# A two-layer encoder on one core: products of ones at the opening, another order of the first casts and loads, a sum moved to VectorE, and the last columns in two runs

## The chip, the core and the metric

The kernel runs on one core of a Trainium2 chip. A core has five engines that each work through their own list of instructions: TensorE (PE in the profile; its weight loads are PEld), VectorE (DVE), ScalarE (ACT), GpSimd (POOL) and SyncE (SP), which here only starts DMA transfers. ScalarE and GpSimd start transfers too (rows ACTq and POOL DMA). The metric is the device time of one execution in microseconds.

## The reference

Two layers work on 256 tokens of 1024 features in float32. Each normalises its input, projects it with one large matrix `w_in` to queries, keys and values of two mixers and to gates, runs both mixers, merges them with sigmoid gates and projects the result back with `w_out`, with a residual. A last normalisation closes.

```python
def rmsnorm(x, w):
    xf = x.astype(jnp.float32)
    y = xf * lax.rsqrt(jnp.mean(xf * xf, axis=-1, keepdims=True) + EPS)
    return y.astype(x.dtype) * w

for l in range(DEPTH):                      # DEPTH = 2
    h = rmsnorm(x, norm_w[l])
    proj = h @ w_in[l]                      # 1024 x 10272
    (q_a, k_a, v_a, ab_a, z_a, q_b, k_b, v_b, z_b,
     gate_a, gate_b) = jnp.split(proj, SPLIT_IDX, axis=-1)
    y_a = gated_delta_branch(q_a, k_a, v_a, ab_a, z_a, ...)   # short convolution, gated delta rule
    y_b = diff_attention_branch(q_b, k_b, v_b, z_b, ...)      # differential attention
    merged = (jax.nn.sigmoid(gate_a) * (y_a @ w_pa[l])
              + jax.nn.sigmoid(gate_b) * (y_b @ w_pb[l]))
    x = x + merged @ w_out[l]
return rmsnorm(x, final_norm_w)
```

## The kernel before

The 256 tokens are two token tiles of 128 (`m` is 0 or 1), the 1024 features eight slices of 128 (`kt`). Every projection is made of column groups of 512. A product in full precision is made of three in the faster format: both operands are split into a high and a low part, and high x high, high x low and low x high are summed in PSUM. So each group of 512 columns takes 2 x 8 x 3 = 48 products of 128 x 128 by 512.

`weights` (L207) loads such a group in four weight blocks (`kp` 0 to 3, 512 KB each, two `kt` in each), casts each to the high part on ScalarE (L230) and subtracts it from the original on VectorE for the low part (L232). The tile `raw` of a load comes free once its low part is made; three such tiles go round, so the fourth load waits for the first subtraction. `later` names an instruction behind which a block's cast or subtraction is to be placed, `held` one behind which its load is issued, on ScalarE's queue instead of SyncE's. `behind(ins)` does the placing: what stands under it is put later in order than `ins`. All else is ordered by a planner that builds each engine's list from a simulated timeline.

`proj_by_tile` (L259) makes the first projection of a layer (group `vb`, tile names `pp_vb`) and the last (`pp_o`) token tile by token tile: all 24 products of tile 0 (L282), then `evac`, then tile 1. For the opening of layer 0, `between` (L363) interleaves this with the norm of the tokens: the load of block 1 goes behind the first square of token tile 0, that of block 2 behind block 0's cast, block 3 by SyncE, and token tile 1's norm follows. The loads after these in the opening are `wab` (L468, behind the cast of block 2, on ScalarE's queue), `cwr` (the rows of the convolution weights, 120 x 128 numbers, L413, on SyncE's queue), and the weights of the k group (`raw_k`, SyncE's).

A norm (`normed`, L172) squares two halves of 512 columns on ScalarE with a sum along the row (L169), adds the two sums and EPS on GpSimd (L164), raises to the power -0.5 on GpSimd (L165), and scales on VectorE (L179). `split_T` (L184) turns the result on TensorE (four transposes of 128 x 128, L189), casts it to the high part on ScalarE (L195) and makes the low part on VectorE (L196); the result is `hT`. In layer 0 the norm's weights come to all rows by a product of one row of ones with the weights' row (`norm_row`, L145, PSUM tile `wb_n`).

At the end, the residual of token tile 1 is added (L1015), squared, summed and raised as above, ScalarE scales the first 512 columns (L1045), VectorE the last (L1046), and two transfers carry the rows out (L1048).

## Time and profile before

| what | value |
|---|---|
| time, median of 3 runs | 779.53 us (779.36 to 779.75) |
| span of the profiled execution, first to last instruction | 777.1 us |
| TensorE busy | 758.2 us, 98% |
| VectorE, ScalarE, GpSimd busy | 557.3, 474.9, 101.9 us |
| DMA | 126.91 MB, mean 163 GB/s |

The page gives the profiled execution by its span; the runs' times take in 2.4 us more, what lies around the first and last instruction. The rows of the timeline give start, length, engine, line, operation, written tile <- read tiles, shapes, and in brackets the idle time before and what ended it. A row of n instructions (xn) spans all of them. The chain of waits follows the work that ended last back to the start: each piece is what the next one waited for.

### The profile page before, as it was taken

The page shows a single profiled execution, that of the slowest core. Times are in us where ns is not written, and L with a number is a line of the kernel's source. Part 1 is how long each engine was busy: PE and PEld are TensorE (multiplying, and loading weights), DVE is VectorE, ACT ScalarE, POOL GpSimd, SP SyncE. Part 2 cuts the span into 40 slices and gives each one's busy share as a digit, 9 for nine tenths or more (in the row PEclk, how much of TensorE's full clock was granted, in tenths as well). Part 3 has the DMA queues.
Part 4 walks back from the last instruction along what each step waited for, and adds up shares of the span by engine and source line. Part 5 has one row for each costly group of instructions (what it writes and reads, how often), then busy time and mean ns, then how long its engine had stood idle before and what let it go on. Part 6 is the DMA issues. An engine that isn't in the chain of part 4 may idle for free.

```text
span 777.1 us, 13805 instructions
## 1 busy us (share of the span) xinstructions
PE 758.2 (98%) x5222; PEld 647.7 (83%) x5222; DVE 557.3 (72%) x1051; ACT 474.9 (61%) x1042; POOL 101.9 (13%) x137
## 2 busy tenths in 40 slices
PE   8999999999999999999999999999999999999996
PEld 4899879887778888887889888899777788888784
DVE  5686878999974635377677776989999553536782
ACT  5657776557677744564554668655577776356551
POOL 5100461100030100010010025510001110001000
PEclk9999999999999999999999999999999999999998
DMA  7752756554496644346664256755446954343631
GB/s 227 240 177 78 224 146 198 174 172 136 112 207 187 210 135 129 117 144 210 215 224 136 82 160 221 194 170 161 141 137 174 233 164 160 114 133 111 213 110 54
DMA packets 77745, 126.91 MB, mean 163 GB/s; under 512 B 19679, under 2 KB 20015, under 8 KB 77680
## 3 DMA queue, kind: packets, MB, share of 16 engines
q1 hardware_dynamic: 71038, 112.99, 48.4%
q0 software_dynamic: 3936, 9.77, 4.8%
q10 hardware_dynamic: 2706, 3.28, 1.3%
q8 instruction: 41, 0.67, 0.4%
q14 instruction: 24, 0.20, 0.1%
HBM read 121.27 MB, written 4.75 MB: 162 GB/s over the span
## 4 chain that ended last, share of the span: by engine, by line
PE 81%; DVE 7%; DMA 5%; ACT 4%; issue 2%; POOL 0%; SPq 0%; POOLq 0%; ACTq 0%; DVEq 0%
PE pp_vb L282 5%; DMA raw_q<-in_w_in_dram 3%; PE pp_qk L245 2%; PE pp_qk L246 2%; PE pp_qk L244 2%; PE pp_o L282 2%; PE pf_k L298 2%; PE pf_k L302 2%; PE pf_v L298 2%; PE pf_k L300 2%; PE pp_gb L245 2%; PE sc L839 2%; PE pp_gb L244 2%; PE pf_v L302 2%; PE pf_v L300 2%; PE av L865 2%
## 5 line engine op out<-in xcount | busy, mean ns | idle before, releaser
L245 PE MATMUL pp_qk<-lo_qk,hT 128*128 128x512 f32 x128 | 51.3, 401 | 1.0 <-DVE lo_qk L232 1.0
L246 PE MATMUL pp_qk<-hi_qk,hT 128*128 128x512 f32 x128 | 50.1, 391 | 0.0
L230 ACT CAST hi_qk<-raw_qk 128x1024 fp32r<-128x1024 f32 x32 | 33.5, 1046 | 23.6 <-PE pp_qk L246 12.6
L244 PE MATMUL pp_qk<-hi_qk,hT 128*128 128x512 f32 x128 | 46.1, 398 | 0.7 <-ACT hi_qk L230 0.7
L232 DVE TENSOR_TENSOR lo_qk<-raw_qk,hi_qk 128x1024 fp32r<-128x1024 f32 x32 | 40.2, 1257 | 7.6 <-ACT hi_qk L230 7.4
L232 DVE TENSOR_TENSOR lo_pb<-raw_pb,hi_pb 128x1024 fp32r<-128x1024 f32 x16 | 19.6, 1224 | 35.7 <-ACT hi_pb L230 35.7
L298 PE MATMUL pf_q<-hT,hi_q 128*128 128x256 f32 x128 | 36.5, 288 | 0.3 <-ACT hi_q L230 0.2
L298 PE MATMUL pf_v<-hT,hi_v 128*128 128x256 f32 x128 | 36.5, 289 | 0.0
L300 PE MATMUL pf_v<-hT,hi_v 128*128 128x256 f32 x128 | 36.2, 286 | 0.0
L300 PE MATMUL pf_q<-hT,hi_q 128*128 128x256 f32 x128 | 35.9, 284 | 0.0
L848 ACT ACTIVATE es<-sc,mx 128x256 f32<-128x256 f32 x64 | 29.8, 473 | 10.1 <-DVE mx L846 10.0
L298 PE MATMUL pf_k<-hT,hi_k 128*128 128x256 f32 x128 | 35.8, 285 | 0.0
L302 PE MATMUL pf_q<-hT,lo_q 128*128 128x256 f32 x128 | 35.7, 292 | 0.0
L300 PE MATMUL pf_k<-hT,hi_k 128*128 128x256 f32 x128 | 35.7, 283 | 0.0
L232 DVE TENSOR_TENSOR lo_gb<-raw_gb,hi_gb 128x1024 fp32r<-128x1024 f32 x16 | 19.6, 1224 | 22.2 <-ACT hi_gb L230 22.0
L232 DVE TENSOR_TENSOR lo_ga<-raw_ga,hi_ga 128x1024 fp32r<-128x1024 f32 x16 | 19.6, 1226 | 21.0 <-ACT hi_ga L230 21.0
L302 PE MATMUL pf_v<-hT,lo_v 128*128 128x256 f32 x128 | 34.6, 286 | 0.0
L302 PE MATMUL pf_k<-hT,lo_k 128*128 128x256 f32 x128 | 34.4, 285 | 0.0
L230 ACT CAST hi_pb<-raw_pb 128x1024 fp32r<-128x1024 f32 x16 | 16.8, 1049 | 25.1 <-PE pp_pb L246 24.3
L527 DVE SCALAR_TENSOR_TENSOR cvq<-pf_q,cw,cvq 128x254 f32<-128x254 f32 (+1 forms) x64 | 29.7, 476 | 1.8 <-ACT cvq L523 1.4
L527 DVE SCALAR_TENSOR_TENSOR cvv<-pf_v,cw,cvv 128x254 f32<-128x254 f32 (+1 forms) x64 | 30.2, 483 | 0.6 <-ACT cvv L523 0.5
L527 DVE SCALAR_TENSOR_TENSOR cvk<-pf_k,cw,cvk 128x254 f32<-128x254 f32 (+1 forms) x64 | 28.5, 478 | 2.0 <-ACT cvk L523 1.3
(356 smaller groups left out, 2495.5 us busy)
## 6 DMA issues: line engine op xcount, KB each, us to landing
raw_qk<-in_w_in_dram SPq DMA_DIRECT2D x32, 512.0 KB, 3.7
raw_k<-in_w_in_dram SPq DMA_DIRECT2D x16, 512.0 KB, 4.6
raw_q<-in_w_in_dram SPq DMA_DIRECT2D x16, 512.0 KB, 3.7
raw_v<-in_w_in_dram SPq DMA_DIRECT2D x16, 512.0 KB, 3.8
raw_zb<-in_w_in_dram SPq DMA_DIRECT2D x16, 512.0 KB, 3.6
raw_za<-in_w_in_dram SPq DMA_DIRECT2D x16, 512.0 KB, 3.7
raw_gb<-in_w_in_dram SPq DMA_DIRECT2D x16, 512.0 KB, 4.7
raw_o<-in_w_out_dram SPq DMA_DIRECT2D x16, 512.0 KB, 4.5
```

Of the source, the lines that this page charges most:

```text
L230: high = S.copy(hi[:, :, :n], raw[:, :, :n]).ins
L232: mark[nm, kp] = high, V.tensor_tensor(lo[:, :, :n], raw[:, :, :n], hi[:, :, :n].bitcast(F32), ALU.subtract).ins
L244: T.matmul(o, act[kt // 4][:, 0, kt % 4, ts_], hi, start=kt == 0, stop=False)
L245: T.matmul(o, act[kt // 4][:, 0, kt % 4, ts_], lo, start=False, stop=False)
L246: mark["proj"] = T.matmul(o, act[kt // 4][:, 1, kt % 4, ts_], hi, start=False, stop=kt == KT - 1).ins
L282: mark["proj"] = T.matmul(o, a_, w_, start=kt == 0 and a_ is ah and w_ is hi, stop=kt == KT - 1 and a_ is al).ins
L298: T.matmul(o, hi[:, cs], act[kt // 4][:, 0, kt % 4, :], start=first, stop=False, skip_group_check=True)
L300: T.matmul(o, hi[:, cs], act[kt // 4][:, 1, kt % 4, :], start=False, stop=False, skip_group_check=True)
L302: T.matmul(o, lo[:, cs], act[kt // 4][:, 0, kt % 4, :], start=False, stop=done, skip_group_check=True)
L527: V.scalar_tensor_tensor(ca[:, o0:o1], acc[:, b, o0 + sft : o1 + sft], cw[:, j, cb : cb + 1], ca[:, o0:o1], ALU.mult, ALU.add)
L839: mm = T.matmul(sp[n][:, qt * SEQ : (qt + 1) * SEQ], qkT[h // 4][rows, 0, h % 4, qt * P : (qt + 1) * P], qkT[h // 4][rows, 1, h % 4, :], s ...
L848: S.activation(es[:, n, qt, :], spv[:, qt, :], AF.Exp, bias=mx[:, n, qt : qt + 1], accum_out=s_all[:, h, n, qt : qt + 1])
```

## The change

Seven edits:

- `ones`, a tile of 128 x 128, is filled on VectorE before the first load, and TensorE multiplies it by itself five times into a PSUM tile that nobody reads.
- The sum of the two mean squares and EPS goes from GpSimd to VectorE, placed behind the same instruction as the squares.
- In layer 0's first projection, block 0 is cast and subtracted in two halves of one `kt` each (`fine`), and its casts are placed behind the cast of the first half of token tile 0 (`split, 0, 0`). Block 2's load and others that name block 0's cast now name its second half.
- In layer 0, the load of the convolution's rows is placed behind the load of block 3 of the first projection.
- In the last projection of layer 1, token tile 1 (`cut`) is made in two runs of 256 columns, each with all 24 products and a residual add of its own.
- The final norm of token tile 1 follows these runs: behind the first, its square, a sum on GpSimd and the product with the weights; behind the second, square, sum on VectorE, power, and the scaling, in which VectorE scales the two quarters by two instructions.
- The tile of the row sums has three columns instead of two.

```diff
     def norm_factor(xt_, m, h, r, ss, halves_, after=None):
...
-        G.tensor_scalar(r, ss[:, 0:1], ss[:, 1:2], EPS, ALU.add, ALU.add)
+        with behind(after):
+            V.tensor_scalar(r, ss[:, 1:2], ss[:, 0:1], EPS, ALU.add, ALU.add)
         mark["pow"] = G.tensor_tensor(r, r, mhalf[:, :1], ALU.pow).ins
...
                 with behind(load):
-                    (nc.scalar if load else nc.sync).dma_start(
+                    mark[nm, "load"] = (nc.scalar if load else nc.sync).dma_start(
                         out=raw[:, :, :n],
...
-                with behind(act):
-                    high = S.copy(hi[:, :, :n], raw[:, :, :n]).ins
-                with behind(dve):
-                    mark[nm, kp] = high, V.tensor_tensor(lo[:, :, :n], raw[:, :, :n],
-                                                         hi[:, :, :n].bitcast(F32), ALU.subtract).ins
+                for ks in ((slice(0, 1), slice(1, 2)) if kp in fine else (slice(0, 2),)):
+                    with behind(act):
+                        high = S.copy(hi[:, ks, :n], raw[:, ks, :n]).ins
+                    with behind(dve):
+                        mark[nm, kp] = high, V.tensor_tensor(lo[:, ks, :n], raw[:, ks, :n],
+                                                             hi[:, ks, :n].bitcast(F32), ALU.subtract).ins
...
-        parts = weights(w, c0, 512, nm, places, ahead=False, later=later, spare=spare, held=held)
+        parts = weights(w, c0, 512, nm, places, ahead=False, later=later, spare=spare, held=held,
+                        fine=(0,) if between else ())
...
+            if m in cut:
+                for c_ in range(2):
+                    cs = slice(256 * c_, 256 * c_ + 256)
+                    for kt in range(KT):
+                        hi, lo = (w_[:, cs] for w_ in ws[kt][1:])
+                        ah, al = (act[kt // 4][:, part, kt % 4, ts_] for part in range(2))
+                        for a_, w_, n_ in ((ah, hi, 0), (ah, lo, 1), (al, hi, 2)):
+                            with behind(mark.get("proj")):
+                                mark["proj"] = T.matmul(o[:, cs], a_, w_, start=kt == 0 and n_ == 0,
+                                                        stop=kt == KT - 1 and n_ == 2).ins
+                    evac(m, o, cs)
+                    yield
+                continue
...
+    ones = work.tile([P, P], F32, tag="sqj", name="ones", bufs=1)
+    V.memset(ones, 1.0)
+    idle = bank_c("idle")
+    for _ in range(5):
+        T.matmul(idle[:, :P], ones, ones, start=True, stop=True)
     wb = norm_row(norm_w[0], "n0")
...
-            later[0] = None, mark["norm", 0][1]
+            later[0] = mark["split", 0, 0][0], mark["norm", 0][1]
...
-        nc.sync.dma_start(out=cw_rows, in_=conv_w[l].rearrange("t (b c) -> (t b) c", c=P))
+        with behind(None if l else mark["vb00", "load"]):
+            nc.sync.dma_start(out=cw_rows, in_=conv_w[l].rearrange("t (b c) -> (t b) c", c=P))
...
+                              cut=() if more else (1,))
...
+                m = min(s_, 1)
                 h, r, ss = outs[m]
                 hv = h.rearrange("p (i d) -> p i d", i=2)
-                norm_factor(xt, m, h, r, ss, (1,))
-                S.activation(hv[:, 0], hv[:, 0], AF.Copy, scale=r)
-                V.scalar_tensor_tensor(hv[:, 1], xt[1][:, m, :], r, wb[1], ALU.mult, ALU.mult)
+                if m == 0:
+                    norm_factor(xt, m, h, r, ss, (1,))
+                    S.activation(hv[:, 0], hv[:, 0], AF.Copy, scale=r)
+                    V.scalar_tensor_tensor(hv[:, 1], xt[1][:, m, :], r, wb[1], ALU.mult, ALU.mult)
+                else:
+                    cs = slice(256 * (s_ - 1), 256 * s_)
+                    S.activation(hv[:, 1, cs], xt[1][:, m, cs], AF.Square, scale=DM ** -0.5,
+                                 accum_out=ss[:, s_ : s_ + 1])
+                    if s_ == 1:
+                        G.tensor_tensor(ss[:, 0:1], ss[:, 0:1], ss[:, 1:2], ALU.add)
+                        V.tensor_tensor(hv[:, 1, cs], xt[1][:, m, cs], wb[1][:, cs], ALU.mult)
+                        continue
+                    V.tensor_scalar(r, ss[:, 2:3], ss[:, 0:1], EPS, ALU.add, ALU.add)
+                    G.tensor_tensor(r, r, mhalf[:, :1], ALU.pow)
+                    S.activation(hv[:, 0], hv[:, 0], AF.Copy, scale=r)
+                    V.scalar_tensor_tensor(hv[:, 1, cs], xt[1][:, m, cs], r, wb[1][:, cs], ALU.mult, ALU.mult)
+                    V.tensor_scalar(hv[:, 1, :256], hv[:, 1, :256], r, None, ALU.mult)
```

More of the change, by code (lines that the diff above doesn't have):

```diff
@@ L155, in norm_tiles @@
                 small.tile([P, 1], F32, tag="xr", name=f"xr_{nm}{m}"),
-                small.tile([P, 2], F32, tag="xss", name=f"xss_{nm}{m}"))
+                small.tile([P, 3], F32, tag="xss", name=f"xss_{nm}{m}"))
     def norm_factor(xt_, m, h, r, ss, halves_, after=None):
@@ L205, in behind, with weights @@
         return nullcontext() if ins is None else tc.issue_after(ins)
-    def weights(w, c0, n, nm, homes=(None,) * 4, ahead=True, later=None, spare=(), held=None):
+    def weights(w, c0, n, nm, homes=(None,) * 4, ahead=True, later=None, spare=(), held=None,
+                fine=()):
         for kp in range(4):
@@ L257, in homes, with proj_by_tile @@
                 yield t_[:, k]
[L259 removed]
+    def proj_by_tile(act, w, c0, evac, nm, places, later=None, turn=None, spare=(), held=None, between=None,
+                     cut=()):
         accs = banks2(f"pp_{nm}")
         ws = []
[L265 removed]
+        parts = weights(w, c0, 512, nm, places, ahead=False, later=later, spare=spare, held=held,
+                        fine=(0,) if between else ())
         if between is None:
@@ L1026, in hybrid_encoder @@
                                      2: mT_split, 3: mT_split}, spare=(1, 3),
-                              turn=lambda m: mark["turn", 0, 0] if m and more else None)
+                              turn=lambda m: mark["turn", 0, 0] if m and more else None,
+                              cut=() if more else (1,))
         outs = []
```

13 lines of the change are left out of this document (6 added, 7 removed).

## The prediction

> **What bounds the kernel now.** I read the page first, then the chain of waits in the opening and in the tail, then the timeline of both places.
>
> ```profile
> span 777.1 us, 13805 instructions
> PE 758.2 (98%) x5222; PEld 647.7 (83%) x5222; DVE 557.3 (72%) x1051; ACT 474.9 (61%) x1042; POOL 101.9 (13%) x137
> ...
> PEclk9999999999999999999999999999999999999998
> ...
> PE 81%; DVE 7%; DMA 5%; ACT 4%; issue 2%; POOL 0%; SPq 0%; POOLq 0%; ACTq 0%; DVEq 0%
> ```
>
> TensorE is busy for 98% of the span. The edits touch its first 21 us, the two layers' norms, and its last 19 us. So the sum is that of two ends. In the opening the chain of waits hardly runs through TensorE:
>
> ```profile
> 1.70 6.07 DMA raw_vb<-in_w_in_dram
> ...
> 7.80 4.84 DMA raw_vb<-in_w_in_dram
> ...
> 12.67 4.39 DMA wab<-in_w_in_dram
> ...
> 19.84 0.60 DVE hT L196
> ```
>
> The first column is the start, the second the length. Three loads stand end to end: the first weight block (kp 0), the third (kp 2, issued on ScalarE's queue with the first block's cast), and wab (issued with the third block's cast). What follows them ends at 20.45, when VectorE hands over the low part of token tile 1; TensorE's last wait of the opening ends with it. What these three loads lose or gain moves the kernel; what shortens TensorE's work before 17 us alone does not.
>
> The timeline of the opening, by engine (TensorE, GpSimd, VectorE, ScalarE with its queue, SyncE's queue):
>
> ```profile
> 3.09 3.77 PE L145 MATMUL wb_n<-wr_n,tri 1*128 1x512 f32 x4 [3.09 <-POOL tri L113]
> 6.95 1.97 PE L189 MATMUL pt_h<-ident,h_n 128*128 128x128 f32 x8
> ...
> 16.52 1.04 PE L189 MATMUL pt_h<-ident,h_n 128*128 128x128 f32 x8
> ```
> ```profile
> 5.16 0.30 POOL L164 TENSOR_SCALAR xr_n<-xss_n 128x1 f32<-128x1 f32 x1 [1.88 <-ACT h_n L169]
> 5.54 0.57 POOL L165 TENSOR_TENSOR xr_n<-xr_n,mhalf 128x1 f32<-128x1 f32 x1
> ```
> ```profile
> 6.15 1.56 DVE L179 SCALAR_TENSOR_TENSOR h_n<-xt,xr_n,wb_n 128x512 f32<-128x512 f32 x2 [3.06 <-POOL xr_n L165]
> ```
> ```profile
> 7.79 1.05 ACT L230 CAST wA_vb<-raw_vb 128x1024 fp32r<-128x1024 f32 x1 [2.73 <-DMA raw_vb<-in_w_in_dram]
> 7.80 0.39 ACTq L226 DMA_DIRECT2D raw_vb<-in_w_in_dram  x1
> 8.74 0.58 ACT L195 CAST hT<-pt_h 128x512 fp32r<-128x512 f32 x1
> ...
> 18.64 0.37 ACTq L226 DMA_DIRECT2D raw_vb<-in_w_in_dram  x1
> 18.82 0.58 ACT L195 CAST hT<-pt_h 128x512 fp32r<-128x512 f32 x1
> 19.05 0.49 ACTq L226 DMA_DIRECT2D raw_vb<-in_w_in_dram  x1
> 19.30 1.06 ACT L230 CAST hi_k<-raw_k 128x1024 fp32r<-128x1024 f32 x1
> ```
> ```profile
> 2.17 0.51 SPq L413 DMA_DIRECT2D cwr<-in_conv_w_dram  x1
> 10.12 0.40 SPq L226 DMA_DIRECT2D raw_vb<-in_w_in_dram  x1
> ```
>
> The same eight transposes take 1.97 us at 6.95 and 1.04 us at 16.52: early on, TensorE runs at half pace. The page's row of the granted clock (PEclk) shows nothing of it, so I go by the durations.
>
> **The change part by part: the opening.**
>
> *Sum of the mean squares.* It leaves GpSimd (0.30, with 0.38 from start to start) for VectorE. The nearest rows for a small operation there, followed by a power on GpSimd, are these (minimum/median/maximum in ns, first and last start):
>
> ```profile
> L569 DVE TENSOR_SCALAR kh<-ge x2: 166/166/167, 76.5 to 454.9; 128x16 f32<-128x16 f32 x2
> ```
> ```profile
> L570 POOL TENSOR_TENSOR nrm<-kh,phalf x2: 2931/2931/2931, 76.8 to 455.2; 128x16 f32<-128x16 f32 x2
> ```
>
> 76.5 to 76.8 is 0.3 from start to start, so each norm gains about 0.1: r comes at 6.05 rather than 6.15. In the other norms but the last this is covered by TensorE's running products, and I count 0. On VectorE the waiting sum holds up what is behind it; at 12 us the next thing there waits for the third block anyway.
>
> *Products of ones.* Five of 128 columns. The norm weights' two products appear as four pieces, so five make ten, each a quarter of 512 columns. The four took 3.77, some 0.9 each, so ten cost 10 x 0.22 = 2.2 us. They can start once VectorE has filled the tile (I estimate 1.1, as its engines begin near 0.8) and end near 3.3, and the norm-weight products that now start at 3.09 start 0.1 to 0.4 later. Those end near 6.9 now, just when the first transposes start. So what r gains, the ones take: transposes still at about 6.9. Bounds of this edit: +0.4, if nothing else waits less, and a gain if the clock rises earlier (rival 2). I take 0.
>
> *First cast behind the high part of tile 0, in halves.* The cast of block 0 now starts at 7.79, as the load lands. After the change it stands behind the hT cast, which needs the first four transposes: half of 1.97 after 6.95, so about 8.0. Two halves of 512 columns cost 0.58 each (the hT row) against 1.05: +0.1 on ScalarE. The first product then starts at 8.0 + 0.58 + 0.58 = 9.2 and its low part follows in halves. TensorE gets ahead by about 0.5, but stands again before block 2, so this by itself is worth 0. What counts is the load of block 2. It is issued behind the second half cast. ScalarE's last four rows say when: there two loads tied to the cast at 19.30 left at 18.64 and 19.05, while the cast still stood in line behind the hT casts. So the issue goes when the cast is dispatched, about 8.05, not when it runs (9.2). That is +0.25 against 7.80.
>
> *The loads.* conv's rows, 60 KB, move from 2.17 to behind the load of block 3 on SP's queue (10.12 before), ahead of the k weights.
>
> ```profile
> DMA packets 6303, 9.36 MB, mean 234 GB/s; under 512 B 1614, under 2 KB 1918, under 8 KB 6301
> ```
> ```profile
> DMA to landing us min/median/max: 3.6/5.4/9.2
> ```
>
> 60 KB at 234 GB/s is 0.26 us of transfer that no longer stands among blocks 0 and 1 and tile 1's rows. Block 3's load also leaves later, since its buffer is free only after two half subtractions (9.2 + 2 x 0.69 = 10.6, not 10.12), so it shares less with block 2. Block 2's load took 4.84; the quickest of its kind took 3.6. I take the middle, 4.2: landing at 8.05 + 4.2 = 12.25 instead of 12.64, -0.4. Bounds: 11.65 to 12.9, so -1.0 to +0.25. The conv rows now stand near wab's 128 KB: between 0 and +0.26, I take +0.1. SP's next loads wait for buffers freed at 11.83 and lose nothing. Opening: -0.3, bounds -1.0 to +0.5.
>
> **The tail.**
>
> ```profile
> 763.89 5.45 PE pp_o L282 x24
> ```
> ```profile
> 769.37 0.69 DVE L1015 SCALAR_TENSOR_TENSOR xt<-pp_o,xt 128x512 f32<-128x512 f32 x1 [2.08 <-PE pp_o L282]
> 770.09 0.63 ACT L169 ACTIVATE h_nf<-xt 128x512 f32<-128x512 f32 x1 [2.83 <-DVE xt L1015]
> 770.63 0.19 ACT L169 ACTIVATION_READ_ACCUMULATOR h_nf<-xt 128x1 f32 x1
> 770.92 0.30 POOL L164 TENSOR_SCALAR xr_nf<-xss_nf 128x1 f32<-128x1 f32 x1 [4.41 <-ACT h_nf L169]
> 771.30 0.57 POOL L165 TENSOR_TENSOR xr_nf<-xr_nf,mhalf 128x1 f32<-128x1 f32 x1
> 771.90 0.72 ACT L1045 ACTIVATE h_nf<-h_nf,xr_nf 128x512 f32<-128x512 f32 x1 [1.09 <-POOL xr_nf L165]
> 771.90 0.75 DVE L1046 SCALAR_TENSOR_TENSOR h_nf<-xt,xr_nf,wb_n 128x512 f32<-128x512 f32 x1 [1.84 <-POOL xr_nf L165]
> ```
>
> The first row is of the chain of waits, the rest is the timeline; all of it stands end to end, and the outputs leave when the last two rows end. Tile 1's 24 products become 48 of 256 columns. Products of that width follow each other so:
>
> ```profile
> 28.06 0.28 PE L302 MATMUL pf_k<-hT,lo_k 128*128 128x256 f32 x1
> 28.18 0.28 PE L298 MATMUL pf_k<-hT,hi_k 128*128 128x256 f32 x1
> ```
>
> 48 x 0.12 = 5.76 against 24 x 0.227 = 5.45: +0.31. Behind the last product only 256 columns remain:
>
> ```profile
> L531 ACT ACTIVATE thq<-cvq 128x256 f32<-128x256 f32 x16 | 6.6, 415 | 3.4 <-DVE cvq L527 3.4
> ...
> L536 DVE SCALAR_TENSOR_TENSOR kq<-thk,cvk 128x256 f32<-128x256 f32 x16 | 6.7, 420 | 4.1 <-ACT thk L531 4.1
> ```
>
> Residual add 0.69 to 0.42 or, reading PSUM, a little more, 0.45: -0.24. Square 0.63 to 0.42, read-out kept: -0.21. Sum on VectorE: -0.1. The last scaling becomes two on VectorE, 0.42 and then 0.17 (the 16-column row above) to 0.42 for the plain multiplication: 0.6 to 0.85 against 0.75, I take +0.05; ScalarE's half (512 columns) is unchanged. The first run's add, square, GpSimd sum and weight product are hidden by the second run's 24 x 0.12 = 2.9 us. Tail: -0.2, bounds -0.4 to 0.
>
> **The sum.** Against the profiled execution: -0.3 - 0.2 = -0.5, a span of 776.6. The median of the runs, 779.53, lies 2.4 above the span of the profile, and so I forecast 779.0.
>
> **The rivals.**
>
> *1. Slower: block 2's load leaves when the half cast runs.* Then it leaves at 9.2, and lands 3.6 to 4.84 later, at 12.8 to 14.0: +0.2 to +1.4, with the conv rows' +0.26, and with the transposes 0.4 later behind the ones up to +2.1 in the opening; less 0.2 in the tail. Time 779.5 to 781.4. For: the issue at 7.80 stands 0.01 behind the start of its cast. Against: the rows at 18.64 and 19.30. It decides against the change from an issue at about 8.5 on.
>
> *2. Faster: the ones raise TensorE's pace before the transposes.* Then eight transposes take 1.04 and their first four end 0.5 sooner, at 7.5; block 2 leaves at 7.55 and lands at 11.15 to 12.4, and wab follows: -0.2 to -1.5. If the wait for VectorE's hT (0.7, below) goes too, up to -2.2; with the tail 777.1 to 779.1, and below 777.97 in the better half. For: the ones use all rows of the array, as the steady products do. Against: 3.77 us of one-row products ending just before did not bring the full pace, and the ones last 2.2.
> The Trainium skill, "TensorE: Matmul & The Clock Gate", Part 1, says that the array starts at half clock and is released after a busy window of about 3.4 us that does not begin with the kernel. By that rule the ones and the products behind them, 5.8 us on end, would release it by 1.1 + 2 x 3.4 = 7.9 at the latest, an estimate, and the time would be rival 2's. The trace agrees on the half pace, but not plainly on the release: products and transposes from 3.09 to 8.9 with little idle time left the pace low, so either one-row products and transposes do not count or more is needed.
>
> *3. Nothing in the opening moves.* wab's chain starts from a landing that stays at 12.6. Only the tail's -0.2 is left: 779.3.
>
> *4. The planner's order shifts in the middle.* A wait of TensorE by place (total, times, longest):
>
> ```profile
> PE pp_vb L282 <- DVE hT L196: 0.7, 1, 0.7
> ```
>
> All instructions are placed by a planner that sees the new opening. Three such waits more or fewer in the middle give 776.9 to 781.1, or 781.3 with a tail that gains nothing. For: the page shows no slack on TensorE. Against: the loads and casts there are not edited.
>
> **How the numbers follow.** Forecast 0.24 and rival 3 0.13, all within 0.2% (777.97 to 781.09, about what a measurement of this kernel can tell from no change). Rival 2 0.30, of which 0.24 below 777.97, since it takes the wait for hT with it in most orders. Rival 1 0.17, of which 0.10 over 781.09. Rival 4 0.16, half on either side. So faster 0.24 + 0.08 = 0.32, slower 0.10 + 0.08 = 0.18, and 0.50 between. Forecast and rival 3 lie 0.3 apart and share their mechanism, so the point stays 779.0. Range 776.9 to 781.4: the lower ends of rivals 2 and 4, the upper of 1 and 4. The forecast's own range is 778.1 to 780.0: its opening's bounds with its tail's.
>
> **What would show it.** Right: the chain of the opening still runs through block 0 or the transposes, block 2 and wab; block 2's issue stands at about 8.0, before its half cast starts at 8.6; wab lands 0.1 to 0.4 sooner; the last product starts 0.3 later from its tile's first, and from there to the last output's issue it takes 2.8 instead of 3.3. Wrong: eight transposes in about 1.0 at 7 us (rival 2), block 2's issue at 9 (rival 1), a chain of the opening through TensorE, or a middle whose stages differ in length.

## The result, and the profile after

| | before | changed |
|---|---|---|
| time, median of 21 runs each | 779.30 us (777.54 to 780.27) | 780.63 us (778.43 to 781.88) |
| ratio to before, 95% interval | | 1.0016 [1.0009, 1.0023] |
| ratio in a second comparison (11 and 35 runs) | | 1.0009 [0.9994, 1.0023] |
| span of the profiled execution | 777.1 us | 777.9 us (its own time 779.69) |

The changed kernel is slower by 0.7 to 1.8 us where 0.5 less was forecast: the sign was wrong, though the size stays near what can be told from no change. The two profiled executions differ by 0.85 us of span, and three places make it up: the opening +0.77, the tail +0.71, and a middle that gives 0.63 back.

The page of the changed kernel, head and first group:

```profile
span 777.9 us, 13880 instructions
PE 760.7 (98%) x5256; PEld 652.1 (84%) x5256; DVE 559.3 (72%) x1062; ACT 476.5 (61%) x1045; POOL 99.0 (13%) x132
```

Its chain of waits in the opening (start, length, what):

```profile
1.11 2.50 PE idle L342 x10
3.62 3.71 PE wb_n L145 x4
7.33 1.06 PE pt_h L190 x4
...
9.53 3.78 DMA raw_vb<-in_w_in_dram
...
13.34 4.62 DMA wab<-in_w_in_dram
...
20.52 0.70 DVE hT L197
```

The load of block 2 leaves at 9.53 instead of 7.80. Once under way it is quicker (3.78 us against 4.84), so it lands 0.67 later; wab's load takes 4.62 against 4.39 and lands 0.90 later, and the last wait ends 0.77 later (token tile 1's third product starts at 21.26, before at 20.49). Why the issue is late is seen in the timeline of the changed kernel, ScalarE and its queue:

```profile
8.41 0.59 ACT L196 CAST hT<-pt_h 128x512 fp32r<-128x512 f32 x1 [3.17 <-PE pt_h L190]
8.89 1.14 ACT L233 CAST wA_vb<-raw_vb 128x512 fp32r<-128x512 f32 x2
9.53 0.39 ACTq L228 DMA_DIRECT2D raw_vb<-in_w_in_dram  x1
9.93 1.05 ACT L233 CAST wktm_vb<-raw_vb 128x1024 fp32r<-128x1024 f32 x1
```

and in the row of block 1's load (issued at 3.90; the last number is the us from issue to landing):

```profile
raw_vb<-in_w_in_dram ACTq DMA_DIRECT2D x1, 512.0 KB, 5.6
```

3.90 + 5.6 = 9.50: the issue at 9.53 goes when block 1 has landed. Here it also stands 0.12 behind the start of the second half cast (about 9.41), but other profiles part the two: in `halves_only`, below, the half casts start at 8.80 and 9.32, block 1 lands at 10.04, and the issue goes at 10.07. In ScalarE's list of the changed kernel the cast of block 1 (`wktm_vb`) stands between the half casts and the issue. It is itself run only at 9.93, but the trace fits only if it isn't dispatched before its data are there, and the issue stands behind it. In the meantime the DMA engines have little to do. Two kernels, the same stretches (start:end, length, busy time of TensorE, weight loads, VectorE, ScalarE, GpSimd, then granted clock, DMA share, GB/s); first before:

```profile
core 0: us, PE busy (x) PEld busy (x) DVE busy (x) ACT busy (x) POOL busy (x), PEclk, DMA share, GB/s
7.00:9.00 2.00, 1.92 (x8) 1.43 (x8) 0.84 (x2) 1.21 (x2) 0.00 (x0) 1.00 1.08 391
9.00:11.00 2.00, 1.63 (x3) 0.83 (x4) 2.00 (x3) 2.00 (x4) 0.00 (x0) 1.00 0.84 262
```

and changed:

```profile
7.00:9.00 2.00, 2.00 (x9) 1.43 (x8) 0.75 (x1) 0.59 (x2) 0.00 (x0) 1.00 0.88 312
9.00:11.00 2.00, 1.70 (x5) 0.82 (x4) 1.89 (x3) 2.00 (x4) 0.00 (x0) 1.00 0.45 121
```

From 7 to 11 us 1.3 MB came in before (2 x 391 + 2 x 262 KB), 0.9 MB after. That these missing bytes make the opening's end late is not shown: `after_prio`, below, fills the gap and ends no sooner.

The tail of the changed kernel, timeline:

```profile
766.49 0.75 DVE L1073 SCALAR_TENSOR_TENSOR h_nf<-xt,xr_nf,wb_n 128x512 f32<-128x512 f32 x1 [0.67 <-POOL xr_nf L166]
767.15 0.42 DVE L1039 SCALAR_TENSOR_TENSOR xt<-pp_o,xt 128x256 f32<-128x256 f32 x1
...
767.63 1.69 PE L284 MATMUL pp_o<-wkq_o,mT 128*128 128x256 f32 x12 [0.73 <-DVE xt L1039]
...
770.79 0.42 DVE L1039 SCALAR_TENSOR_TENSOR xt<-pp_o,xt 128x256 f32<-128x256 f32 x1 [2.17 <-PE pp_o L284]
...
773.50 0.39 ACTq L1088 DMA_DIRECT2D out_dram<-h_nf  x1
```

From the last product to the last output's issue the work is shorter as forecast: 770.79 to 773.50 is 2.71 us, before it was 769.37 to 772.65, 3.28. But TensorE stands for 0.73 us between the two runs, waiting for VectorE's residual add of the first run. That add comes late because VectorE is on the scaling of token tile 0 (766.49), and TensorE waits for it because both runs write the same PSUM tile. "Tail" in the table below is the time from tile 1's first product to that last issue: 8.93 before, 9.64 after.

In the middle the planner has put TensorE's work on the heads of layer 0 into another order, though nothing there was edited. One row shows it, 32 products of the projection `pa` (number, min/median/max ns, first to last start). Before, in layer 1 and in layer 0, and then changed, in layer 0:

```profile
L244 PE MATMUL pp_pa<-hi_pa,yaT x32: 389/389/483, 721.5 to 745.8; 128*128 128x512 f32 x32
L244 PE MATMUL pp_pa<-hi_pa,yaT x32: 389/390/484, 343.1 to 367.4; 128*128 128x512 f32 x32
```
```profile
L247 PE MATMUL pp_pa<-hi_pa,yaT x32: 389/389/393, 346.0 to 368.0; 128*128 128x512 f32 x32
```

In layer 0 they start 2.9 later and end 0.6 later; they take 22.0 us from first to last instead of 24.3, with no long one among them. The order of layer 1 is that of before.

### The profile page after: what moved, and what is told of

Its sections match the earlier page's. It is cut to its first block, busy times and chain, and to the rows that moved or that the text cites. A ratio compares the mean times of both kernels' runs of the same rounds, so it can differ in the third digit from the quotient of the medians.

```text
span 777.9 us, 13880 instructions
## 1 busy us (share of the span) xinstructions
PE 760.7 (98%) x5256; PEld 652.1 (84%) x5256; DVE 559.3 (72%) x1062; ACT 476.5 (61%) x1045; POOL 99.0 (13%) x132
## 3 DMA queue, kind: packets, MB, share of 16 engines
q10 hardware_dynamic: 2706, 3.28, 1.3%
## 4 chain that ended last, share of the span: by engine, by line
PE 80%; DVE 8%; ACT 5%; DMA 4%; issue 2%; POOL 0%; POOLq 0%; ACTq 0%; DVEq 0%
PE pp_vb L300 4%; PE pp_qk L248 3%; PE pp_qk L249 3%; PE pp_qk L247 2%; PE pf_v L316 2%; ACT B L652 2%; PE sc L863 2%; PE pf_v L320 2%; PE pf_v L318 2%; PE pp_gb L247 2%; PE pp_gb L249 2%; PE pp_gb L248 2%; PE pp_pb L248 2%; PE pp_pb L249 2%; PE pp_pb L247 2%
```

## The experiments

All were timed beside before, `halves_spare` by four executions, the other kernels by 7 to 12, the changed one of the first comparison by 21. None leaves out a part of the computation. "Third product" is the start of tile 1's third product in the opening, from the profile; "issue" that of block 2's load; "order" says in which layers TensorE's heads stand in the other order.

| kernel | time, before (us) | ratio, 95% interval | issue | third product | tail | order |
|---|---|---|---|---|---|---|
| before | | | 7.80 | 20.49 | 8.93 | |
| changed | 780.63, 779.30 | 1.0016 [1.0009, 1.0023] | 9.53 | 21.26 | 9.64 | 0 |
| `after_again` | 779.40, 779.68 | 1.0009 [0.9994, 1.0023] | 8.80 | 21.38 | 9.64 | 0 |
| `opening_only` | 779.19, 779.84 | 0.9996 [0.9982, 1.0010] | 8.42 | 21.03 | 8.75 | 0 |
| `tail_only` | 780.26, 779.84 | 0.9999 [0.9988, 1.0010] | 7.99 | 20.55 | 9.83 | |
| `tail_two_banks` | 779.32, 779.84 | 0.9989 [0.9978, 1.0001] | 7.00 | 20.39 | 8.66 | |
| `no_ones` | 780.45, 779.84 | 1.0005 [0.9996, 1.0015] | 8.88 | 21.58 | 9.65 | 0 |
| `halves_only` | 778.13, 779.78 | 0.9977 [0.9966, 0.9988] | 10.07 | 21.14 | 8.93 | 0, 1 |
| `conv_only` | 779.39, 779.78 | 1.0002 [0.9993, 1.0011] | 7.67 | 20.36 | 8.93 | |
| `ones_only` | 779.54, 779.78 | 0.9997 [0.9985, 1.0009] | 8.12 | 21.39 | 8.93 | |
| `best` | 778.57, 779.78 | 0.9990 [0.9978, 1.0002] | 7.89 | 20.95 | 8.66 | 1 |
| `after_two_banks` | 778.82, 779.68 | 0.9993 [0.9982, 1.0004] | 8.84 | 21.05 | 8.66 | 0 |
| `halves_two_banks` | 778.33, 779.68 | 0.9983 [0.9971, 0.9995] | 9.51 | 21.27 | 8.66 | 0, 1 |
| `halves_early` | 778.66, 779.68 | 0.9992 [0.9980, 1.0004] | 5.66 | 23.68 | 8.66 | 0, 1 |
| `sum_only` | 778.48, 779.96 | 0.9987 [0.9976, 0.9997] | 7.82 | 20.73 | 8.76 | 1 |
| `after_prio` | 781.02, 779.96 | 1.0016 [1.0007, 1.0026] | 8.41 | 21.44 | 9.64 | |
| `halves_prio` | 777.10, 779.96 | 0.9967 [0.9954, 0.9979] | 8.67 | 20.59 | 8.66 | 0, 1 |
| `halves_spare` | 782.84, 779.96 | 1.0039 [1.0021, 1.0057] | 12.61 | 25.50 | 8.66 | |
| `hp_conv` | 777.53, 779.66 | 0.9971 [0.9959, 0.9983] | 8.27 | 21.18 | 8.66 | 0, 1 |
| `hp_ones` | 779.02, 779.66 | 0.9992 [0.9982, 1.0002] | 8.40 | 21.20 | 8.66 | |

**The change in two.** `opening_only` is the changed kernel without the tail's two runs:

```diff
-                              cut=() if more else (1,))
+                              cut=())
```

with the last norm as before but for its sum on VectorE.

> All of the change but its tail: token tile 1 of the last projection is again made in one run of 512 columns, with the tail of before. Theory A (two losses, one in the opening from a late load of block 2, one in the tail from a stall of TensorE): from TensorE's first product of tile 1 on, the opening is 0.8 us late, as in the changed kernel, and the tail is as long as before, so +0.5 to +0.9 us. Rival (the opening's delay is given back in the middle and the tail costs it all): within 0.2 us of before.

`tail_only` is before with nothing but the two runs and the norm that follows them.

> The kernel before with only the tail in two runs and its norm. Theory A: the opening is as before, and from the last projection's tile 1 to the last output's issue it takes 0.7 us more than before, with an idle time of TensorE of about 0.7 us between the two runs, released by VectorE's residual add; time +0.5 to +0.8 us. Rival (the opening alone made the change slower): -0.2 us or no difference.

Without the two runs the change costs nothing that can be told, 0.9996; the tail alone measured 0.9999. By time both ratios lie nearer to the rivals than to the theory, and neither interval is narrow enough to lay the blame. The profiles show where: the tail alone takes 9.83 instead of 8.93, with a wait of 0.92 between the runs (0.73 in the changed kernel).

```profile
768.47 1.70 PE L280 MATMUL pp_o<-wkq_o,mT 128*128 128x256 f32 x12 [0.92 <-DVE xt L1029]
```

**Two PSUM tiles.** The second run gets a PSUM tile of its own, on before plus the tail (`tail_two_banks`) and on the changed kernel (`after_two_banks`):

```diff
+                both = [o, banks2(f"pq_{nm}")[0]]
                 for c_ in range(2):
                     cs = slice(256 * c_, 256 * c_ + 256)
+                    o = both[c_]
```

> As tail_only, but the second run of 256 columns goes to a PSUM tile of its own. If TensorE waited because both runs share one tile, the idle time of 0.7 us between the runs is gone, the second run ends 0.7 to 0.9 us sooner, and the time is 0.2 us under before. Rival (it waited for something else, or the narrower products are what costs): as slow as tail_only, +0.5 us or more.

> The changed kernel, with the second run of the last tile in a PSUM tile of its own. Theory (the tail's loss is the stall behind the first run's residual add): tail 8.66 instead of 9.64, no wait of TensorE between the two runs, and 0.8 to 1.0 us faster than the changed kernel, 779.5 where before is 779.5. Rival (the two runs of 256 columns themselves cost it): tail 9.2 or more, less than 0.4 us faster.

Both profiles have a tail of 8.66. The tail of `after_two_banks`:

```profile
766.32 1.60 PE L286 MATMUL pp_o<-wB_o,mT 128*128 128x256 f32 x12
...
767.76 1.60 PE L286 MATMUL pq_o<-wkq_o,mT 128*128 128x256 f32 x12
768.18 0.42 DVE L1041 SCALAR_TENSOR_TENSOR xt<-pp_o,xt 128x256 f32<-128x256 f32 x1
...
770.84 0.42 DVE L1041 SCALAR_TENSOR_TENSOR xt<-pq_o,xt 128x256 f32<-128x256 f32 x1 [1.18 <-PE pq_o L286]
```

The add still comes late (768.18, behind tile 0's scaling), but TensorE no longer waits for it. So the loss in the tail is the shared tile: 9.64 - 8.66 = 0.98 us. On the same chip the ratio went from 1.0009 to 0.9993 and the median from 779.40 to 778.82, about the size expected, though the two intervals overlap. The rival, that the runs of 256 columns themselves cost it, falls: from tile 1's first product to the last add it takes 764.89 to 770.84, 5.95, and before 763.73 to 769.37, 5.64, which is the +0.31 of the prediction.

**Single edits of the opening.** `no_ones` is the changed kernel without the products of ones, `ones_only` before with them, `conv_only` before with the conv rows behind block 3, `halves_only` before with the first cast in halves behind the hT cast:

```diff
-        parts = weights(w, c0, 512, nm, places, ahead=False, later=later, spare=spare, held=held)
+        parts = weights(w, c0, 512, nm, places, ahead=False, later=later, spare=spare, held=held,
+                        fine=(0,) if between else ())
...
-            later[0] = None, mark["norm", 0][1]
+            later[0] = mark["split", 0, 0][0], mark["norm", 0][1]
```

> The change without the five products of ones. If the ones delay the norm weights' products and with them all of the opening, the transposes start 0.4 us sooner than in the changed kernel (near 6.9), and the issue of block 2's load moves from 9.53 to about 9.1, if it follows the casts, or stays at 9.5, if it waits for block 1 to land; time 0.4 us or 0 below the changed kernel. Rival (the ones raise TensorE's pace): the opening gets longer without them.

> The kernel before with only the five products of ones. They delay the norm weights' products by 0.5 us and the transposes by 0.3 to 0.4. If the opening hangs on loads and casts that do not wait for the transposes, the third product of tile 1 starts within 0.2 us of 20.5, time unchanged. If the ones raise TensorE's pace, the first eight transposes take 1.0 instead of 2.0 us.

> The kernel before with only the load of conv's rows moved behind block 3's load. Rival to theory B: wab's cast starts at 17.6 or later, 0.5 to 1 us later than before, the third product of tile 1 at 21 or later. Theory B: wab's cast at 17.0 to 17.4, the product near 20.5; the first loads are up to 0.3 us sooner.

> The kernel before with only block 0's cast behind the hT cast and in halves. Theory B (the late subtraction of block 0 frees its buffer late, so block 3's load, and with it wab's landing and TensorE's third product of tile 1, come late): block 3's load leaves at 10.7 to 11 instead of 9.3 to 10.3, wab's cast starts at 17.8 to 18.3 instead of 17.0 to 17.15, the third product of tile 1 at 21.0 to 21.5 instead of 20.4 to 20.55. Rival (the conv rows beside wab are what delays it): wab's cast near 17.1, the product near 20.5.

In `conv_only` the rows are neutral by time and by profile. With the halves alone the issue stands at 10.07 and the third product at 21.14. That is in theory B's range, but not by its path: wab's cast starts at 17.32 where 17.8 or later was expected, and the chain of waits comes from block 3's landing at 15.24 through VectorE. With the ones alone the issue is near its old place (8.12), and the third product still comes at 21.39, where within 0.2 of 20.5 was expected. In `no_ones` the issue goes at 8.88, again with block 1's landing (8.85), and the third product at 21.58 is no sooner than with the ones. In all seven profiles with ones it lies between 21.03 and 21.44, in the six with neither ones nor halves between 20.36 and 20.95; with halves and without ones it comes at 21.14 to 21.58 in four and at 20.59 in one (`halves_prio`, below; two more, which load otherwise, are told of there). So either edit can go with a late end, and together they cost no more. Yet the time of `ones_only` is that of before (0.9997), and `halves_only` is 1.7 us faster than before in spite of its opening. It has the other order of the heads, in both layers, and the next kernels ask what that gains.

**The order of the heads.** `sum_only` changes only the engine of a sum; its opening is that of before, and TensorE's order differs in layer 1 alone.

```diff
-        G.tensor_scalar(r, ss[:, 0:1], ss[:, 1:2], EPS, ALU.add, ALU.add)
+        with behind(after):
+            V.tensor_scalar(r, ss[:, 1:2], ss[:, 0:1], EPS, ALU.add, ALU.add)
```

> Before, with only the sum of the mean squares on VectorE. The sum itself is worth 0.1 per norm; but with it the planner orders TensorE's heads of layer 1 (about 610 to 720 us) otherwise. Theory (that order is worth 0.8, as in halves_only and best; and the last norm gives 0.18): 0.8 to 1.1 us faster than before, ratio 0.9986 to 0.9990, and the shift against before falls by about 0.8 between 610 and 740 us. Rival (the order of the middle is worth nothing; those kernels gained by chance): 0 to 0.2 faster, 0.9997 to 1.0001.

It is faster by 0.9987 [0.9976, 0.9997], about 1.0 us (0.2 to 1.9), of which the tail's sum can be 0.17 (8.93 to 8.76). The row of layer 1's `pa` in `sum_only`, beside the one of before at 721.5 to 745.8 above:

```profile
L245 PE MATMUL pp_pa<-hi_pa,yaT x32: 389/389/393, 722.6 to 744.6; 128*128 128x512 f32 x32
```

It starts 1.1 later and ends 1.2 sooner. The same products, measured against before just ahead of the heads and just behind them, say what the order is worth in a profile. In layer 1 the kernels in the old order moved by -0.83 to +0.84 (mean of 13, before's own 0 among them: -0.37), those in the other order by -1.24, -1.24, -1.24, -1.23 and -1.04, and by +0.34 and +0.37 where TensorE's clock was halved for 3.4 us there (below). In layer 0 the old order moved by -0.51 to +0.89 (mean of 10, 0 included: +0.05), the other by -0.96 to +0.34 (mean of nine: -0.60, a tenth left out where the clock was halved). The difference of the means is 0.65 in layer 0 and 0.8 in layer 1. All three stretches left aside for their halved clock lie in the other order; with them kept in the means, the difference is 0.4 in each layer. Whether the other order brings the halved clock more often is open, and so is where its gain comes from: TensorE's waits by place add up to no less in it. Nor does it account for all of `halves_only`: 0.65 + 0.8, less some 0.6 in the opening, is 0.8 to 0.9 us, and 1.8 (0.9 to 2.7) were measured.

`best` joins that sum with the tail in two PSUM tiles.

> The opening of before but with the sums on VectorE; the tail in two runs with a PSUM tile for each. The tail takes 8.5 to 8.7 us from tile 1's first product to the last output's issue, 0.25 to 0.4 less than before; the opening is as before; time 0.3 us (0.04%) below before and about 1.5 below the changed kernel. Rival (VectorE's sum holds up its queue): the third product of tile 1 later than 20.7.

The ratio 0.9990 [0.9978, 1.0002] is about what layer 1's order and the tail would make, but not clear of no change. The third product at 20.95 is what the rival said, later than 20.7; in `sum_only`, with the same sum, it came at 20.73. `halves_two_banks` joins the halves, with both layers' order, to that tail:

> Before, with only the first cast in halves behind hT and the last tile in two runs with two PSUM tiles. Theory (the gain of halves_only, -1.65, is the planner's other order in the middle and stays; the tail gives 0.27 more): 1.3 to 2.0 us faster than before, ratio 0.9975 to 0.9984. Rival (halves_only was fast by chance, its opening costs 0.6 and its middle nothing): ratio 0.9997 to 1.0005.

0.9983 [0.9971, 0.9995] is within what the order's theory gave, and clear of its rival's.

**The changed kernel again.**

> The changed kernel once more, on the chip of the next three kernels. Theory (opening +0.6, tail +0.7, reordered middle of layer 0 -0.8, and a part not found): ratio to before 1.0005 to 1.002; from the first product of tile 1 of the last projection to the last output's issue 9.6; tile 1's third product of the opening at 21.0 to 21.5; block 2's load issued at the landing of block 1, 8.4 to 10, whenever the half casts run. Rival (the changed kernel is no slower than before; the first comparison was chance): 0.9990 to 1.0002.

The tail and the opening's end come out as in the first profile, the issue at 8.80 with block 1's landing (3.55 + 5.2 = 8.75), here ahead of both half casts (8.89 and 9.41). This time block 2 landed at 12.45, sooner than before (12.64), and the third product came at 21.38 all the same: wab took 5.6 us instead of 4.4. The ratio 1.0009 holds the theory and, within its interval, the rival too.

**The issue of block 2.** `halves_early` issues it behind the second square of tile 0, ahead of all casts:

```diff
-                held[2] = mark["vb00", 0][0]
+                held[2] = mark["square", 0, 1]
```

> As halves_two_banks, but the load of block 2 is issued on ScalarE's queue behind the second square of tile 0, so ahead of the casts that wait for blocks 0 and 1. Theory (the opening's +0.6 is the later issue of block 2, behind block 1's landing): block 2 issued at 5 to 6, tile 1's third product of the opening at 20.6 or sooner instead of 21.1, 0.4 to 0.8 us faster than halves_two_banks. Rival (the three loads share the same transfer rate, so an earlier issue only stretches them): block 2 lands within 0.3 of before, blocks 0 and 1 land later by 0.5 to 1, third product at 21 or later, no gain.

`halves_spare` gives block 3 another buffer, so that its load leaves at once, and names the hT cast for the issue of block 2:

```diff
-                              spare=(1, 3) if l else (), held=held, between=between,
+                              spare=(1, 3) if l else (3,), held=held, between=between,
```

> As halves_two_banks, but the first projection's last block (block 3) is loaded into another buffer, so it waits for nothing and is issued at about 2.3 on SyncE's queue instead of 10.8; TensorE's order is that of before in the middle. Theory (in the opening the transfers share one rate, about 290 GB/s in this stretch; more bytes early only push out what is needed first): blocks 0 and 1 and tile 1's rows land 0.5 to 1.5 later, no wait for wab at the end or a smaller one, third product between 20 and 22. Rival (the queues run dry, so an earlier issue is pure gain): blocks 0 and 1 land as before and the third product comes at 19 or sooner.

Neither gains. In `halves_early` the early issue buys little: wab, issued once block 2 has landed, leaves at 11.99 instead of 12.67 before, and takes 5.7 us instead of 4.4; and the planner puts wab's cast ahead of block 3's on ScalarE, so that TensorE waits 2.9 us for block 3 and then runs at half clock for 3.4 us. Its profile was among the slowest of its executions (780.29 us): by the median it is 0.3 us behind `halves_two_banks`, which is no difference that can be told, in place of the gain expected.

```profile
PE pp_vb L300 <- ACT wB_vb L231: 2.9, 1, 2.9
```

In `halves_spare` block 1 takes 8.67 us, in the other kernels 4.4 to 6.1 (rows of the chain of waits), and the issue of block 2 again waited for block 1's landing (12.58) and went at 12.61:

```profile
3.90 8.67 DMA raw_vb<-in_w_in_dram
...
12.61 4.52 DMA raw_vb<-in_w_in_dram
```

That is the theory's mechanism, with a loss of 5.0 in the opening where up to 1.5 was expected, and 1.0039 by time. Here the bytes that left early pushed out those that were needed first.

`after_prio` is the changed kernel with the issue placed where the prediction had seen it, right behind the hT cast; `high_priority` moves it ahead in the planner's order:

```diff
-                with behind(load):
+                with behind(load), (tc.high_priority(offset=HP) if load and kp == 2 else nullcontext()):
...
-                held[2] = mark["vb00", 0][0]
+                held[2] = mark["split", 0, 0][0]
```

> The changed kernel, with the load of block 2 placed right behind the cast of hT on ScalarE's queue, ahead of the half casts and of the cast that waits for block 1. With it the planner keeps the old order of layer 0's heads. Theory (block 2's late issue is the opening's loss, the other order of layer 0 is worth 0.8): issue at 8.2 to 8.4, no dry stretch of the DMA engines at 9 to 11 us, tile 1's third product at 20.4 to 20.9 instead of 21.3; shift against before flat from 230 to 350 us instead of falling by 0.4 to 0.7; so in time 0 to 0.4 slower than the changed kernel. Rival (the middle's order is worth nothing): 0.4 to 0.9 faster than the changed kernel. Second rival (the ones, not the issue, cost the opening): third product at 21.2 or later, as with the ones alone.

`halves_prio` is `halves_two_banks` with the same edit.

> As halves_two_banks, with the load of block 2 placed right behind the cast of hT on ScalarE's queue; no ones, conv rows as before. Both layers' heads stay in the other order. Theory: block 2 issued at 8.2 to 8.4 instead of 9.5, third product at 20.3 to 20.8 instead of 21.2, 0.4 to 0.8 faster than halves_two_banks, so 1.7 to 2.2 faster than before, ratio 0.9972 to 0.9978. Rival (the opening's loss is not the issue): as halves_two_banks, 0.9983.

In `after_prio` the issue stands at 8.41, though block 1 lands only at 9.72: with the cast of block 1 behind it, it no longer waits. The dry stretch is gone (226 GB/s from 9 to 11 us, against 121), and block 2 lands at 12.33. But the third product comes at 21.44, as the second rival said and not the theory: wab, issued at 12.36, took 5.8 us. The rows of wab's load, in before, `after_again` and `after_prio` (last number: us to landing):

```profile
wab<-in_w_in_dram ACTq DMA_DIRECT2D x1, 128.0 KB, 4.4
wab<-in_w_in_dram ACTq DMA_DIRECT2D x1, 128.0 KB, 5.6
wab<-in_w_in_dram ACTq DMA_DIRECT2D x1, 128.0 KB, 5.8
```

So in the profile the late issue does not make the changed kernel's opening. With this edit the planner took the old order of layer 0's heads, and the ratio, 1.0016, is no better than the changed kernel's, which is the theory's time. In `halves_prio`, without ones and with the conv rows in their old place, the same edit gives 20.59, with 148 GB/s from 9 to 11 us and a wab that took 5.0. Its chain of waits:

```profile
8.67 0.39 ACT hT L195
...
12.34 4.95 DMA wab<-in_w_in_dram
...
19.85 0.70 DVE hT L196
```

It is faster than before by 0.33% [0.21, 0.46], some 2.6 us, and faster than the changed kernel too. Two more kernels are to tell the ones from the conv rows, each added to `halves_prio`:

> As halves_prio, with the conv rows loaded behind block 3 as in the changed kernel; TensorE's order is that of halves_prio throughout. Theory (conv's 60 KB next to wab's small packets delay wab): wab lands 0.5 to 1 later than in halves_prio, tile 1's third product at 21.1 to 21.5 instead of 20.6, 0.4 to 0.8 slower than halves_prio, ratio to before 0.9972 to 0.9980. Rival (the place of the rows is neutral, as in conv_only): third product at 20.3 to 20.9, ratio 0.9967.

> As halves_prio, with the five products of ones added; with them the planner keeps the old order of the heads in both layers. Theory (the ones push the opening back by 0.3 to 0.9, the old order costs 0.6 per layer): third product at 21.0 to 21.5, and 1.4 to 2.1 slower than halves_prio, so 0.5 faster to 0.3 slower than... before by a ratio of 0.9987 to 0.9997. Rival (the ones are neutral and the order is worth nothing): third product at 20.6, ratio 0.9967.

With the conv rows moved, TensorE's order is that of `halves_prio` throughout, and the ratio 0.9971 against 0.9967 can't be told from it. Its profile has the third product at 21.18, as the theory said, and wab took 5.6; but it is of the slowest of the seven executions (782.62 us), so it says little of the rest. With the ones the ratio is 0.9992, the third product at 21.20: both as expected. But the ones also brought the old order in both layers, so that the 1.9 us to `halves_prio` are of ones and order together.

## Why the prediction was wrong

**The bounds** were right for the changed kernel: the opening's end is set by block 2, wab and what follows, the tail by work end to end, and what changed between them is the planner's order.

**The first cast.** The step that failed: "the issue goes when the cast is dispatched, about 8.05". The rule held: in `opening_only`, where block 1 had landed at 8.22, and in `after_prio`, where the issue stands ahead of block 1's cast, it went at 8.42 and 8.41 with the hT cast, ahead of the half casts at 8.89. But the prediction took the issue to stand "behind the second half cast" and nothing else. The planner put the cast of block 1 in between, and that waits for a landing (8.75 and 9.50 in the changed kernel's two profiles). The delay was 1.0 to 1.7 us instead of 0.25. The prediction's own row at 18.64 had the sign of it: that issue left as the second block of the k group landed (issued at 14.99, 3.6 us to landing), whose cast is the one at 19.30. Rival 1 had the delay and the time (779.5 to 781.4), but by luck: its mechanism did not occur, as `after_again` issues at 8.80, ahead of both half casts, and the tail's loss was not in it.

**The loads.** Block 3 left at 10.95 (10.6 in the prediction) and block 2 took 3.78 (4.2), quicker, as was argued from less sharing. In the first profile block 2 landed at 13.31 instead of 12.25 and wab took 0.23 more where +0.1 was taken; the opening ended 0.77 later where the sum had -0.3 and bounds to +0.5. But the late issue is not all. In `after_again` and `after_prio` block 2 landed at 12.45 and 12.33, near the 12.25 forecast, and the third product came 0.9 and 1.0 later than before. The second step that failed is the size of wab's term, "between 0 and +0.26": there it was +1.2 and +1.4. Why wab takes longer is open. In 19 of the 20 profiles it lands within 0.7 us behind the first block of the k group, whether issued at 11.55 or at 13.92; in the changed kernel that block left at 12.26 instead of 11.86 and landed at 17.59 instead of 16.56, so "lose nothing" did not hold for SP's next loads either. No run moved that load by itself. Over the four profiles with the changed kernel's opening the third product lies at 21.18 on average, over the six with neither ones nor halves at 20.58: +0.6.

**The ones** were no trade against the norm's sum, which gained nothing here: 0.37 from its start to that of the power (0.38 before), and r came at 6.24 instead of 6.15. Ten pieces took 2.50 us instead of 2.2, the norm weights' products start at 3.55 instead of 3.09 (0.1 to 0.4 in the prediction), and the cover was gone: VectorE's second scaling waits for them, and the transposes come at 7.26 instead of 6.95.

```profile
7.26 2.03 PE L190 MATMUL pt_h<-ident,h_n 128*128 128x128 f32 x8
7.36 0.75 DVE L180 SCALAR_TENSOR_TENSOR h_n<-xt,xr_n,wb_n 128x512 f32<-128x512 f32 x1 [0.37 <-PE wb_n L145]
```

The first row, 2.03 against 1.97 before, also settles rival 2: the pace did not rise. What the ones cost in time stays open: nothing that can be told in `ones_only`, and 0.0011 or 0.0004 between the changed kernel's two ratios and that of `no_ones`, with intervals that overlap.

**The sum on VectorE** took 0.29 from its start to that of the power in the last norm (0.3 in the prediction). "In the other norms but the last ... I count 0" left out what the planner makes of it: alone it reorders layer 1 and measured 1.0 us faster (0.2 to 1.9). In the changed kernel that order did not come, but layer 0's did, by rival 4's mechanism. By the means above it gives back about 0.6, or 0.4 with the halved clock kept, and is not in the forecast's sum. In the changed kernel's own profile it can't be told from the rest: its heads moved by -0.29 in layer 0, and by -0.78 in layer 1, where the order is the old one.

**The tail.** +0.31 for the products and -0.57 behind the last one (-0.50 in the prediction) were right, and with two PSUM tiles the tail is worth -0.27 (-0.2). The third step that failed: "The first run's add, square, GpSimd sum and weight product are hidden by the second run's 24 x 0.12 = 2.9 us". The add is not hidden: the second run has to wait for it, as it writes the tile that the add reads. +0.71 instead of -0.2.

**What adds up.** Opening +0.6, tail +0.7, layer 0's order -0.6: +0.7, at the low end of the first interval (0.7 to 1.8) and in the middle of the second (-0.5 to 1.8). Whether the other 0.5 of the first comparison is chance or lies in executions where the longer opening halves TensorE's clock (below) was not shown: neither profile of the changed kernel has such a stretch.

## What to carry to other kernels

When an issue or a cast is moved, write out the list of its engine as the planner will leave it, and ask of each instruction ahead what it waits for: one cast that waits for a landing holds up every transfer issue behind it. A tile's products cut in two runs need two accumulators, or the second run waits for the reader of the first, and that reader for whatever its engine is doing. Where a planner orders everything, a small edit can be worth more by the order that it brings elsewhere than by itself; compare the orders before explaining a time. And take the length of a load from more than one run: wab's was 2.6 to 5.8 us in these profiles.

## What the runs showed of the hardware

TensorE's clock can fall back to half within the kernel. In three profiles (`tail_two_banks`, `hp_conv`, `halves_early`) the granted clock was 0.50 for 3.41 us right behind the opening's waits; in the first two the last product of the first projection then starts 7.6 and 7.5 us after the third product of tile 1 instead of 5.9 to 6.0. Two stretches of `tail_two_banks`, the 3.4 us ahead and that of the drop:

```profile
17.60:21.00 3.40, 1.79 (x8) 0.96 (x7) 3.02 (x7) 3.14 (x5) 2.99 (x6) 1.00 0.55 143
21.00:24.40 3.40, 3.40 (x10) 2.62 (x9) 2.11 (x8) 1.50 (x2) 0.55 (x1) 0.50 0.92 271
```

of `hp_conv`:

```profile
17.90:21.30 3.40, 1.80 (x8) 0.92 (x7) 2.70 (x7) 3.38 (x6) 3.40 (x7) 1.00 0.55 156
21.30:24.70 3.40, 3.40 (x9) 2.66 (x10) 2.63 (x9) 1.77 (x3) 0.69 (x2) 0.50 0.78 169
```

and of `after_again`, where it did not drop:

```profile
17.90:21.30 3.40, 1.85 (x8) 0.90 (x6) 2.50 (x6) 3.19 (x6) 3.40 (x7) 1.00 0.66 184
21.30:24.70 3.40, 3.32 (x17) 2.80 (x18) 3.01 (x12) 1.97 (x4) 0.64 (x2) 1.00 0.56 156
```

TensorE stood for 1.61 and 1.60 us of these 3.4 where the clock fell, and for 1.55 where it stayed. The same happened further on, in `after_prio` at 481 us, behind a wait of 2.0 us for a weight block, in `halves_two_banks` at 621 and in `hp_conv` at 247 and 625 us. Those last three followed stretches of 3.41 us in which TensorE stood for only 1.17, 1.35 and 1.17 us, so the time it stands does not decide alone; what else counts is not shown. It is a likely source of the spread between executions: the profiled one was the slowest of 12 in `tail_two_banks` and the slowest of 7 in `hp_conv`. The Trainium skill, "TensorE: Matmul & The Clock Gate", Part 1, describes a window of 3413 ns that runs freely and so makes the warm-up vary from run to run; the length agrees with the 3.41 us here. It has the clock go cold after one idle window of about 3.4 us; here less than half a window of standing was enough (1.60 and 1.61 of 3.41 us).
